# Rotary embedding on one core: first-tile stores in pieces, and a 64 KB partition step with 2 KB table runs

## The chip, the cores and the metric

The kernel runs on one core of a Trainium2 chip. The metric is device time in microseconds (us); a median over several executions is quoted.

## The reference

```python
batch, seq_len, num_heads, head_dim = (8, 2048, 16, 64)
x1, x2 = x_pairs[..., 0], x_pairs[..., 1]       # neighbours in the last axis
out1 = x1 * cos - x2 * sin
out2 = x1 * sin + x2 * cos                      # interleaved again into the last axis
```

Everything is float32: x and the output are 67.1 MB each, cos and sin 0.26 MB each. The arithmetic is a few operations per element, so what counts is moving 134.7 MB in and out.

## The kernel before

x is cut into 16 tiles of 4 MB. A tile has 128 partitions, and each partition holds K = 8 consecutive sequence rows, one run of 32 KB. In a tile, the next partition's run starts 32 KB further on, so a tile is one contiguous stretch of memory.

```python
P, K, NX = 128, 8, 5
x_t = x.rearrange("b (g p k) h d -> b g p k (h d)", p=P, k=K)
out_t = out.rearrange("b (g p k) h d -> b g p k (h d)", p=P, k=K)
cos_t = cos.rearrange("(g p k) c -> p g (k c)", p=P, k=K)      # two 1 KB runs per partition
first_runs = [(0, 1), (1, 2), (2, 4), (4, 8)]
last_runs = [(0, 4), (4, 6), (6, 7), (7, 8)]

def load_runs(i):
    return first_runs if i == 0 else last_runs if i == n - 1 else [(0, K)]

def store_runs(i):
    return last_runs if i == n - 1 else [(0, K)]
# ... cut: halve() casts a piece to bf16 on ScalarE, rotate() is three VectorE operations ...
def widen(j):
    i, k0, k1 = pieces[j]
    nc.scalar.copy(out=tiles[i][:, k0:k1], in_=rotated.pop(j)[:, : k1 - k0])
    g, b = groups[i]
    for r0, r1 in store_runs(i):
        if r1 == k1:
            nc.scalar.dma_start(out=out_t[b, g, :, r0:r1], in_=tiles[i][:, r0:r1])
    if k1 == K and i + NX < n:
        load(i + NX)          # the same buffer: waits until tile i is stored
# ... cut ...
load(0); <cos and sin>; load(1) ... load(4); <build tables>; <pieces in order>
```

Five tile buffers rotate. Loads are issued from SyncE's queue, stores from ScalarE's. The sixth load, tile 5, needs the buffer of tile 0, so it goes out when tile 0 has been stored.

A packet, below, is one record of the DMA trace: one contiguous run moved by one of the 16 DMA engines.

## Time and profile before

| | before |
|---|---|
| device time | 318.54 us, median of 3 (318.48 to 318.76) |
| bytes moved | 134.76 MB |
| VectorE, ScalarE busy | 70%, 73% |
| DMA rate over the span | 425 GB/s |

These lines are from the page of the kernel before; in the lines of part 5, busy time and mean ns of one stand between the bars, and after the second bar the idle time just before and what ended it.

```profile
span 316.9 us, 352 instructions
DVE 223.2 (70%) x111; ACT 230.0 (73%) x73; POOL 0.2 (0%) x4
DMA packets 6451, 134.76 MB, mean 425 GB/s; under 512 B 689, under 2 KB 1201, under 8 KB 1969
...
L75 ACT CAST xh<-xt 128x4096 bf16<-128x4096 f32 (+2 forms) x36 | 116.1, 3224 | 66.9 <-DMA xt<-in_x_dram 61.6
```

No compute engine is full, and ScalarE waits 61.6 us for loads. The windows view of the same kernel shows what fills the time: start:end and length of each stretch, busy time of VectorE, ScalarE and GpSimd, clock, share of the 16 DMA engines, GB/s.

```profile
0.00:3.00 3.00, 0.00 (x0) 1.28 (x1) 0.20 (x4) 1.00 0.38 90
3.00:19.00 16.00, 4.36 (x8) 3.15 (x4) 0.00 (x0) 1.00 1.06 442
19.00:36.00 17.00, 15.26 (x10) 15.15 (x6) 0.00 (x0) 1.00 1.00 432
36.00:98.00 62.00, 58.20 (x26) 59.80 (x17) 0.00 (x0) 1.00 1.00 430
98.00:176.00 78.00, 55.24 (x26) 57.83 (x18) 0.00 (x0) 1.00 1.00 431
176.00:254.00 78.00, 48.74 (x22) 50.27 (x15) 0.00 (x0) 1.00 1.00 432
254.00:308.00 54.00, 39.32 (x21) 39.49 (x13) 0.00 (x0) 1.00 1.00 431
308.00:312.40 4.40, 2.08 (x3) 3.03 (x3) 0.00 (x0) 1.00 0.97 411
312.40:315.20 2.80, 0.00 (x0) 0.00 (x1) 0.00 (x0) 1.00 0.88 361
```

The DMA share is 1.00 from 19 to 308 us. In short windows it can pass 1.00 (1.06 above), so a per cent or two in one such window is not a difference in rate. The Trainium skill, "DMA: Bandwidth & Descriptors", section "Where 436 GB/s comes from", gives 435 GB/s as the ceiling of the fabric; the trace reaches 431.

Two lines more: the first is from SyncE's queue in the timeline (start, length), the other two from the DMA issues (median us from issue to landing).

```profile
59.78 0.33 SPq L70 DMA_DIRECT2D xt<-in_x_dram  x1
...
out_dram<-xt ACTq DMA_DIRECT2D x1, 1024.0 KB, 11.7
out_dram<-xt ACTq DMA_DIRECT2D x2, 512.0 KB, 4.1
```

The sixth load goes out at 59.78 us.

### The profile page before, as it was taken

How to read it: one execution, taken by the hardware profiler on the slowest of the kernel's cores; microseconds unless marked ns; L12 is line 12 of the kernel's file. 1: busy time of each engine (PE TensorE's matmuls, PEld its weight loads, DVE VectorE, ACT ScalarE, POOL GpSimd, SP SyncE). 2: the span in 40 equal slices, each digit the busy share in tenths (PEclk: the TensorE clock that was granted, in tenths of full speed). 3: DMA queues.
4: the chain of work that ended last, by engine and by line, in shares of the span. 5: the costliest groups of instructions: out<-in, count | busy, mean ns of one | idle time of the engine just before them, and what ended most of it. 6: DMA issues, size and time to landing. Idle time of an engine off the chain costs nothing.

```text
span 316.9 us, 352 instructions
## 1 busy us (share of the span) xinstructions
DVE 223.2 (70%) x111; ACT 230.0 (73%) x73; POOL 0.2 (0%) x4
## 2 busy tenths in 40 slices
DVE  0189999999999596693967939588440999999112
ACT  4078899999998692976949679495803999997322
POOL 0000000000000000000000000000000000000000
DMA  7999999999999999999999999999999999999997
GB/s 304 424 463 405 455 397 401 459 438 422 455 405 463 397 460 401 459 414 448 443 418 455 405 459 405 455 405 459 418 443 447 414 428 430 424 433 439 442 414 302
DMA packets 6451, 134.76 MB, mean 425 GB/s; under 512 B 689, under 2 KB 1201, under 8 KB 1969
## 3 DMA queue, kind: packets, MB, share of 16 engines
q1 hardware_dynamic: 3712, 67.63, 50.1%
q10 hardware_dynamic: 2736, 67.11, 49.1%
q14 instruction: 3, 0.02, 0.0%
HBM read 67.63 MB, written 67.11 MB: 425 GB/s over the span
## 4 chain that ended last, share of the span: by engine, by line
DMA 62%; ACT 26%; DVE 4%; issue 3%; another core or an unknown queue 2%; SPq 1%; ACTq 1%
DMA xt<-in_x_dram 31%; DMA out_dram<-xt 28%; ACT xt L105 14%; ACT xh L75 12%; DMA sin_sb<-in_sin_dram 4%; DVE xh L100 1%; DVE xh L95 1%; DVE qt L94 1%; SPq L70 1%; ACTq L109 1%; DVE s_tab L121 0%; SPq L115 0%; DVE s_tab L122 0%; ACTq L105 0%
## 5 line engine op out<-in xcount | busy, mean ns | idle before, releaser
L75 ACT CAST xh<-xt 128x4096 bf16<-128x4096 f32 (+2 forms) x36 | 116.1, 3224 | 66.9 <-DMA xt<-in_x_dram 61.6
L105 ACT CAST xt<-xh 128x4096 f32<-128x4096 bf16 (+2 forms) x36 | 116.0, 3223 | 14.8 <-DVE xh L100 14.4
L94 DVE TENSOR_TENSOR qt<-xh,s_tab 128x4096 bf16<-128x4096 bf16 (+2 forms) x36 | 74.0, 2055 | 71.2 <-ACT xh L75 70.3
L100 DVE TENSOR_TENSOR xh<-xh,qt 128x4096 bf16<-128x4096 bf16 (+2 forms) x36 | 74.0, 2055 | 1.2
L95 DVE TENSOR_TENSOR xh<-xh,c_tab 128x4096 bf16<-128x4096 bf16 (+2 forms) x36 | 74.0, 2055 | 1.2
L121 DVE CAST s_tab<-sin_sb 128x512 bf16<-128x512 f32 x1 | 0.5, 453 | 14.4 <-DMA sin_sb<-in_sin_dram 14.4
L75 ACT ACT_TABLE_LOAD x1 | 1.3, 1283 | 0.7 <-PEq L147 0.7
L123 DVE CAST c_tab<-cos_sb 128x1024 bf16<-128x1024 f32 x1 | 0.7, 684 | 0.0
L122 DVE TENSOR_SCALAR s_tab<-sin_sb 128x512 bf16<-128x512 f32 x1 | 0.4, 442 | 0.0
L147 POOL MEMSET const-bfloat16-1.0<- 128x1 bf16 x1 | 0.1, 101 | 0.0
L147 POOL MEMSET const-uint8-127<- 128x1 uint8 x1 | 0.1, 101 | 0.0
L147 POOL MEMSET const-float32-0.0<- 128x1 f32 x1 | 0.1, 98 | 0.2 <-issue 0.2
L147 POOL MEMSET const-float32-1.0<- 128x1 f32 x1 | 0.1, 98 | 0.0
## 6 DMA issues: line engine op xcount, KB each, us to landing
out_dram<-xt ACTq DMA_DIRECT2D x15, 4096.0 KB, 38.6
xt<-in_x_dram SPq DMA_DIRECT2D x14, 4096.0 KB, 26.6
xt<-in_x_dram SPq DMA_DIRECT2D x2, 2048.0 KB, 16.3
xt<-in_x_dram SPq DMA_DIRECT2D x4, 512.0 KB, 24.1
xt<-in_x_dram SPq DMA_DIRECT2D x2, 1024.0 KB, 19.9
out_dram<-xt ACTq DMA_DIRECT2D x1, 2048.0 KB, 17.6
out_dram<-xt ACTq DMA_DIRECT2D x1, 1024.0 KB, 11.7
out_dram<-xt ACTq DMA_DIRECT2D x2, 512.0 KB, 4.1
```

The source lines that it names most:

```text
L70: nc.sync.dma_start(out=tiles[i][:, k0:k1], in_=x_t[b, g, :, k0:k1])
L75: nc.scalar.copy(out=halved[j][:, : k1 - k0], in_=tiles[i][:, k0:k1])
L94: nc.vector.tensor_tensor(out=rows(qt), in0=rows(xh), in1=tab(s_tab), op=mult)
L95: nc.vector.tensor_tensor(out=rows(xh), in0=rows(xh), in1=tab(c_tab), op=mult)
L100: nc.vector.tensor_tensor(out=xh3, in0=xh3, in1=q_swap, op=add)
L105: nc.scalar.copy(out=tiles[i][:, k0:k1], in_=rotated.pop(j)[:, : k1 - k0])
L109: nc.scalar.dma_start(out=out_t[b, g, :, r0:r1], in_=tiles[i][:, r0:r1])
L121: nc.vector.tensor_copy(out=s2[:, :, 0], in_=sin_flat)
L122: nc.vector.tensor_scalar_mul(s2[:, :, 1], sin_flat, -1.0)
L123: nc.vector.tensor_copy(out=c_tab.rearrange("p g k (i j) -> p (g k i) j", j=2), in_=cos_sb.rearrange("p g c -> p (g c)").to_broadcast([P, ...
L147: nc = _bacc.Bacc("TRN2", target_bir_lowering=False, num_devices=1)
```

## The change

The intent: start storing the first tile before all of it is done, and read each partition's table rows in one run of 2 KB. To get the second, a partition now holds 16 consecutive rows of a batch row, and two tiles are interleaved over them.

```diff
-    x_t = x.rearrange("b (g p k) h d -> b g p k (h d)", p=P, k=K)
-    out_t = out.rearrange("b (g p k) h d -> b g p k (h d)", p=P, k=K)
-    cos_t = cos.rearrange("(g p k) c -> p g (k c)", p=P, k=K)
-    sin_t = sin.rearrange("(g p k) c -> p g (k c)", p=P, k=K)
+    x_t = x.rearrange("b (p g k) h d -> b g p k (h d)", p=P, k=K)
+    out_t = out.rearrange("b (p g k) h d -> b g p k (h d)", p=P, k=K)
+    cos_t = cos.rearrange("(p k) c -> p (k c)", p=P)
+    sin_t = sin.rearrange("(p k) c -> p (k c)", p=P)
 ...
     def store_runs(i):
-        return last_runs if i == n - 1 else [(0, K)]
+        return load_runs(i)
 ... (cut: the same tables without the g axis)
```

A partition's run of x stays 32 KB, but its neighbour's now starts 64 KB further on.

More of the change, by code (lines that the diff above doesn't have):

```diff
@@ L41 @@
     hpool = ctx.enter_context(tc.tile_pool(name="hpool", bufs=1))
-    cos_sb = consts.tile([P, G, K * D2], fp32)
-    sin_sb = consts.tile([P, G, K * D2], fp32)
+    cos_sb = consts.tile([P, G * K * D2], fp32)
+    sin_sb = consts.tile([P, G * K * D2], fp32)
     c_tab = consts.tile([P, G, K, D], bf16)
@@ L119 @@
         s2 = s_tab.rearrange("p g k (i j) -> p (g k i) j", j=2)
-        sin_flat = sin_sb.rearrange("p g c -> p (g c)")
-        nc.vector.tensor_copy(out=s2[:, :, 0], in_=sin_flat)
-        nc.vector.tensor_scalar_mul(s2[:, :, 1], sin_flat, -1.0)
+        nc.vector.tensor_copy(out=s2[:, :, 0], in_=sin_sb)
+        nc.vector.tensor_scalar_mul(s2[:, :, 1], sin_sb, -1.0)
         nc.vector.tensor_copy(
             out=c_tab.rearrange("p g k (i j) -> p (g k i) j", j=2),
-            in_=cos_sb.rearrange("p g c -> p (g c)").to_broadcast([P, G * K * D2, 2]),
+            in_=cos_sb.to_broadcast([P, G * K * D2, 2]),
         )
```

## The prediction

> **What bounds the kernel now.** The DMA engines, nearly without a gap. The page gives 134.76 MB at a mean of 425 GB/s over a span of 316.9 us; ScalarE is busy 73%, VectorE 70%. The windows view shows a DMA share of 1.00 and 430 to 432 GB/s in each of 19:36, 36:98, 98:176, 176:254 and 254:308 us, and 431 GB/s over 3:315.2. The Trainium skill, "DMA: Bandwidth & Descriptors", section "Where 436 GB/s comes from", puts the fabric ceiling of the 16 engines at 435 GB/s; the trace agrees, at 99% of it. The waits view shows ScalarE waiting 61.6 us for loads and the load queue 242 us for stores: both sides wait for DMA. From 36 to 98 us the chain of waits runs through ScalarE alone, but the DMA share there is 1.00 too, so this costs nothing.
>
> Outside saturation lie only the first 3 us (90 GB/s) and the end: 308:312.4 at 411 GB/s, 312.4:315.2 at 361, and 1.7 us after the last byte. Against 431 GB/s about 2.4 us are lost at the head and 2.4 us at the end. This is all that any reordering could win.
>
> **What the change does.**
> 1. The first tile's single 4 MB store, issued at 35.9 us, becomes four, at about 19, 22, 27 and 36 us (the ends of its widening copies in the timeline). But from 19 to 36 us the DMA engines already run at 432 GB/s on loads. Some 2 MB of stores move forward and push 2 MB of loads back; the sum is the same. The sixth load, issued at 59.8 us once this store has landed, should go out 5 to 10 us earlier. Gain at the end: about 0. Cost: three more issues of 0.34 us on ScalarE's queue, where there is slack (12.7 us of waiting right after 98 us).
> 2. The tables come in 256 packets of 2 KB instead of 512 of 1 KB: 0.5 MB, 1.2 us of DMA time at 431 GB/s. I estimate at most 0.2 us saved.
> 3. Not named in the words of the change: a partition's runs of x and out stay 32 KB, but the step between partitions becomes 64 KB instead of 32 KB; tiles are no longer one contiguous 4 MB. The same page, "Latency and other measured facts", reports a 3% loss at an HBM row pitch of 512 KiB and far more at 2 MiB; 64 KiB is below what it lists. I expect no loss; no run has shown it yet.
>
> Instructions, shapes and order on VectorE are unchanged.
>
> **Predicted time:** 318.3 us, 8 times in 10 between 317.0 and 319.8. Chances: faster by over 2%: 1%; within 2%: 96%; slower by over 2%: 3%.
>
> **What the profile would show.** Span near 316.7. The windows between 19 and 308 us at 430 to 432 GB/s; 134.76 MB moved. Four first-tile stores from about 19 us. The sixth load issued nearer 50 us. ScalarE's wait for loads within 10 of 61.6 us. Packets under 2 KB fewer by about 512. The last load lands 7 to 9 us before the last byte.
>
> **What would make it wrong.** A steady rate below 425 GB/s at the 64 KB step (each 1% lost costs 3 us), or one nearer 435 (2 to 3 us won). Or fewer bytes of stores are queued when the last load lands (3 MB now), so that the DMA engines idle during the last chain of 4.3 us (308.1 to 312.4): 1 to 2 us lost.

## More of the kernel before

A 4 MB tile is 128 packets of 32 KB; a piece of one sequence row per partition (512 KB) is 128 packets of 4 KB. Every transfer ends with a 4-byte completion packet on each engine.

## The result, and the profile after

| | before | after |
|---|---|---|
| device time, median | 318.56 us (318.48 to 318.76, 4 runs) | 318.86 us (318.71 to 319.03, 4 runs) |
| ratio | | 1.0009, 95% interval 0.9991 to 1.0026 |
| profiled span | 316.9 us | 316.9 us |

A ratio is the mean time of one kernel's fast runs over that of the other's from the same rounds, so it is not quite the ratio of the medians quoted. The interval includes 1: no difference is shown.

The page of the changed kernel, the lines that answer to those above:

```profile
span 316.9 us, 352 instructions
DVE 223.2 (70%) x111; ACT 230.3 (73%) x73; POOL 0.2 (0%) x4
DMA packets 6626, 134.76 MB, mean 425 GB/s; under 512 B 736, under 2 KB 736, under 8 KB 2016
...
L76 ACT CAST xh<-xt 128x4096 bf16<-128x4096 f32 (+2 forms) x36 | 116.1, 3225 | 67.7 <-DMA xt<-in_x_dram 61.1
```

The windows view of the changed kernel, the same stretches and columns:

```profile
0.00:3.00 3.00, 0.00 (x0) 1.28 (x1) 0.20 (x4) 1.00 0.40 68
3.00:19.00 16.00, 3.95 (x7) 2.70 (x3) 0.00 (x0) 1.00 1.05 438
19.00:36.00 17.00, 14.21 (x10) 14.54 (x7) 0.00 (x0) 1.00 0.98 419
36.00:98.00 62.00, 58.25 (x27) 59.74 (x18) 0.00 (x0) 1.00 1.01 434
98.00:176.00 78.00, 56.44 (x25) 58.44 (x17) 0.00 (x0) 1.00 1.00 432
176.00:254.00 78.00, 48.16 (x22) 50.26 (x15) 0.00 (x0) 1.00 1.00 432
254.00:308.00 54.00, 40.14 (x21) 40.30 (x13) 0.00 (x0) 1.00 1.00 430
308.00:312.40 4.40, 2.08 (x3) 2.67 (x3) 0.00 (x0) 1.00 0.98 416
312.40:315.20 2.80, 0.00 (x0) 0.37 (x1) 0.00 (x0) 1.00 0.88 360
```

Bytes, busy times and rates are the same; the 1 KB packets are gone. The 419 in 19:36 is an effect of the window's edges: with each packet's bytes spread over its own duration, 7.34 MB were moved in that stretch before and 7.32 MB after.

The timeline of SyncE's queue and the DMA issues of the changed kernel did not do what was predicted:

```profile
63.59 0.33 SPq L71 DMA_DIRECT2D xt<-in_x_dram  x1
...
out_dram<-xt ACTq DMA_DIRECT2D x4, 512.0 KB, 10.1
out_dram<-xt ACTq DMA_DIRECT2D x2, 1024.0 KB, 20.3
```

The sixth load goes out 3.8 us later than before, at 63.59 us, although its buffer's store was started 16 us earlier (first piece at 19.47 us). The median time to landing of the 512 KB stores is 10.1 us instead of 4.1, because two of the four are now first-tile pieces.

The trace's packet records, cumulated by queue (MB moved by each time), show why:

```
us                      24     28     32     36     40     44     48     60
before, load queue    9.14  10.87  12.60  14.33  15.94  16.78  17.30  20.27
before, store queue   0.00   0.00   0.00   0.00   0.00   0.75   1.96   4.19
after,  load queue    8.95  10.48  12.02  13.56  15.10  16.63  17.90  21.50
after,  store queue   0.08   0.28   0.47   0.65   0.84   1.04   1.40   2.99
```

From 24 to 44 us the store queue of the changed kernel gets about 0.19 MB in 4 us, the load queue 1.53 MB: one ninth of the total, and a 4 KB packet beside a 32 KB packet is 4/36, one ninth. Between 28 and 36 us, 91 load packets of 32 KB and 91 store packets of 4 KB start. The two queues take turns packet by packet, and a turn is worth what its packet holds. The Trainium skill, same page, section "Queues, rings and completion order", says that each engine goes round robin between its queues at packet granularity; this trace agrees, 91 to 91. (The page gives a packet as typically 9 to 17 descriptors. Here one turn is one packet record, one partition's run; how many descriptors make up a record the trace does not show.)

So the four pieces of the first tile were complete at 34.7, 45.8, 57.9 and 63.0 us, the whole tile of before at 59.4 us: the early pieces did arrive earlier, but the last one, which frees the buffer, arrived later.

In the kernel before, both queues carried 32 KB packets once the store began. Between 44 and 48 us the store queue got 1.21 MB of 1.73: 32 of its packets started beside 16 of the load queue, whose other 16 turns went to 4-byte completion packets. A completion packet takes a turn too.

### The profile page after: what moved, and what is told of

Its sections match the earlier page's. It is cut to its first block, busy times and chain, and to the rows that moved or that the text cites. A ratio compares the mean times of both kernels' runs of the same rounds, so it can differ in the third digit from the quotient of the medians.

```text
span 316.9 us, 352 instructions
## 1 busy us (share of the span) xinstructions
DVE 223.2 (70%) x111; ACT 230.3 (73%) x73; POOL 0.2 (0%) x4
## 4 chain that ended last, share of the span: by engine, by line
DMA 72%; ACT 16%; DVE 4%; issue 3%; another core or an unknown queue 2%; SPq 1%; ACTq 1%
DMA out_dram<-xt 37%; DMA xt<-in_x_dram 32%; ACT xt L106 9%; ACT xh L76 7%; DMA sin_sb<-in_sin_dram 4%; DVE xh L101 1%; DVE xh L96 1%; DVE qt L95 1%; SPq L71 1%; ACTq L110 1%; SPq L116 0%; DVE s_tab L121 0%; DVE s_tab L122 0%; DVE c_tab L123 0%
## 5 line engine op out<-in xcount | busy, mean ns | idle before, releaser
L76 ACT CAST xh<-xt 128x4096 bf16<-128x4096 f32 (+2 forms) x36 | 116.1, 3225 | 67.7 <-DMA xt<-in_x_dram 61.1
## 6 DMA issues: line engine op xcount, KB each, us to landing
out_dram<-xt ACTq DMA_DIRECT2D x4, 512.0 KB, 10.1
```

The lines of the kernel that those rows point to most:

```text
L76: nc.scalar.copy(out=halved[j][:, : k1 - k0], in_=tiles[i][:, k0:k1])
```

## The experiments

All of them are correct unless marked. "By 19 us" means the megabytes that packet records show as moved by then.

**1. The store pieces alone**, on the layout of before.

```diff
     def store_runs(i):
-        return last_runs if i == n - 1 else [(0, K)]
+        return load_runs(i)
```

> Kernel before plus the first tile's store in four pieces; 32 KB step between partitions kept. Theory (the two DMA queues take turns packet by packet, so a 4 KB store packet gets one turn against a 32 KB load packet): the store queue moves at 4/36 = 11% of the total while 4 KB packets stand at its head, about 0.2 MB per 4 us from 24 to 44 us; the sixth load goes out at 63 to 65 us, later than the 59.8 us of before, and the total time is that of before within 0.2 us. Sine rows land at 14.4 us as before. Rival (the 64 KB step or the table layout delayed the sixth load): it goes out at or before 59.8 us here.

Measured: 319.28 us (319.24 to 319.85, 5 runs) against 318.67; ratio 1.0022, interval 1.0009 to 1.0036. From its SyncE timeline:

```profile
64.65 0.33 SPq L70 DMA_DIRECT2D xt<-in_x_dram  x1
```

The sixth load is late without the new layout, and the store queue moves 0.19 MB per 4 us between 24 and 44 us (90 load packets of 32 KB beside 93 store packets of 4 KB from 28 to 36 us). So the pieces delay it, not the step. Two expectations missed: the sine rows landed at 15.2 us, not 14.4 (14.5 in the repetition, experiment 10), and the time rose by 0.6 us, not 0.2 (which did repeat).

**2. The new layout alone**: the changed kernel with the first tile stored whole.

```diff
     def store_runs(i):
-        return load_runs(i)
+        return last_runs if i == n - 1 else [(0, K)]
```

> The changed kernel with the first tile stored whole: 64 KB step and 2 KB table runs alone. Theory: the head is slower by about 0.4 us (first 1 MB of loads, 4 KB packets, mean over 200 ns instead of 190; sine rows land at 14.8 to 15.0 us), the steady windows stay at 430 to 432 GB/s, the sixth load goes out at about 60 us, and the time is 0.2 to 0.5 us over before. Rival (0.3 us of the changed kernel is noise, or comes from the store pieces): the time is that of before within 0.15 us.

Measured: 318.97 us (318.83 to 319.25, 5 runs) against 318.67; ratio 1.0009, interval 0.9996 to 1.0021. From its SyncE timeline and its waits view (us in total, times, longest):

```profile
60.16 0.33 SPq L71 DMA_DIRECT2D xt<-in_x_dram  x1
...
DVE s_tab L121 <- DMA sin_sb<-in_sin_dram: 14.8, 1, 14.8
```

The sixth load is back at 60 us. The head, the first microseconds of the kernel, is slower: 6.93 MB by 19 us instead of 7.03, which is 0.23 us at 431 GB/s (about 0.4 was expected), and the 4 KB packets of the first 1 MB took 210 ns on average instead of 191. The 0.3 us in the total agrees in sign and size, but the interval includes 1.

**3. Smaller load packets beside the store pieces**: the changed kernel with tiles 1 to 4 loaded in quarters, 8 KB packets.

```diff
+        quarters = [(0, 2), (2, 4), (4, 6), (6, 8)]
-        return first_runs if i == 0 else last_runs if i == n - 1 else [(0, K)]
+        return first_runs if i == 0 else quarters if i < NX else last_runs if i == n - 1 else [(0, K)]
```

(Stores of tiles 1 to 4 stay whole.)

> The changed kernel with tiles 1 to 4 loaded in four pieces each, so that the load packets which compete with the first stores are 8 KB instead of 32 KB. Packet-turn theory: the 4 KB store packets now get 4/12 = 33% of the rate, about 0.55 to 0.6 MB per 4 us instead of 0.2, the 8 KB ones half; the first tile's last piece lands near 50 us, and the sixth load goes out when the early loads are done, near 50 us instead of 63.5. Rival (a store piece is slow by itself, by its completion or its 4 KB packets): the store rate stays near 0.2 MB per 4 us and the sixth load near 63 us. Total time: within 1 us of the changed kernel, as the DMA engines stay full.

Measured: 319.89 us (one run, state unknown). From its SyncE timeline:

```profile
49.54 0.33 SPq L72 DMA_DIRECT2D xt<-in_x_dram  x1
```

From 24 to 28 us the store queue moved 0.56 MB and the load queue 1.14 MB: a share of 33%, as 4/12 demands, where it was 11%. The sixth load went out at 49.54 us, 14 us sooner. Same 4 KB store packets, same sizes, another neighbour: a store piece is not slow by itself. The total time did not gain from the earlier load. It was 1.03 us over the changed kernel's 318.86, just outside the 1 us expected. The smaller load packets alone account for about 0.8 us of that: an estimate from the usual duration of each packet size, summed over all packets and divided by 16 engines.

**4. The first tile loaded whole**, on the kernel before.

```diff
     def load_runs(i):
-        return first_runs if i == 0 else last_runs if i == n - 1 else [(0, K)]
+        return last_runs if i == n - 1 else [(0, K)]
```

> Kernel before with the first tile loaded whole (32 KB packets) instead of in four pieces. The tables land after that tile anyway, so the early pieces buy no compute. If the slow head is many small packets: 0.2 to 0.6 us faster, with the sine rows earlier than 14.4 us. If the head is a cost of first touching the memory, whatever the packets: same time within 0.2 us.

Measured: 318.45 us (318.36 to 318.87, 5 runs) against 318.67; ratio 0.9995, interval 0.9982 to 1.0007. The median is 0.2 us lower, the low end of what was expected, but the interval includes 1. By 19 us 7.04 MB instead of 7.03, and the sine rows landed at 14.5 us: nothing that shows was won at the head. At the 32 KB step the small first packets cost no time that shows. They bring no rotation forward either, since the tables land after that tile (the sine rows at 14.4 us); only the first casts to bf16 run early.

**5, 6, 7. A copy in place of the kernel**: the same tiles, buffers and queues, the loaded tile stored unchanged, no tables; with a step between partitions of 32, 64 and 512 KB. Their outputs are wrong, which doesn't matter for the times.

```diff
-    <tables, halve, rotate, widen>
+    for i in range(n):
+        nc.scalar.dma_start(out=out_t[b, g], in_=tiles[i])
+        if i + NX < n:
+            load(i + NX)
 (512 KB: "(p i k) c -> i p k c" on the (b s) rows)
```

> Wrong on purpose: x is loaded and stored unchanged in whole tiles through the same two queues and five buffers, no tables, no arithmetic; 32 KB step. Theory (the packets' time fills the kernel): 4096 packets of 32 KB at 1213 ns on 16 engines are 310.5 us; with the 2 us of head, 1 to 1.5 us of slow first packets and the end, 316.5 to 317.5 us, so all the arithmetic, tables and pieces of the kernel before cost only 1 to 2 us. Rival (the waits for ScalarE or for buffers cost more than the windows show): under 315 us.

> The same copy, wrong on purpose, with the 64 KB step. Theory (the step only slows the first packets): 0.1 to 0.5 us over the copy with the 32 KB step, steady windows equal. Rival (the step costs bandwidth): more than 1 us over it, spread over the span. If the 0.3 us of the changed kernel was noise: equal within 0.1 us.

> The same copy, wrong on purpose, with a 512 KB step (a partition holds 128 consecutive rows, over batch rows). The Trainium skill's page on DMA reports 3% less for that row pitch in copies from HBM to HBM; if this holds for a single pass through SBUF: 3% over the copy with 32 KB, about 326 us. If only the first packets on fresh memory are slow: head excess 2 to 8 times that of the 32 KB step and 317 to 320 us.

| step | median us (range, runs) | ratio to before, 95% interval |
|---|---|---|
| 32 KB | 316.78 (316.65 to 317.0, 6) | 0.9927, 0.9887 to 0.9966 |
| 64 KB | 317.02 (316.47 to 317.1, 6) | 0.9930, 0.9890 to 0.9970 |
| 512 KB | 320.01 (319.22 to 323.61, 4) | 1.0051, 0.9975 to 1.0126 |

Before had a median of 318.67 in these rounds; one of its 11 runs, at 323.13, widens the intervals.

The 32 KB copy is the floor of this design, and the kernel before is 1.9 us above it. The packet durations account for that: at their usual durations (the median for each size) the kernel before's packets take 312.7 us of 16 engines, the copy's 310.6. Of the 2.1 us between them 1.5 are the tables (512 packets of 46 ns over 16 engines), and nearly all of the rest is the smaller packets of the first and last tile. No cost is left over for the arithmetic.

The ranges of the 32 and 64 KB copies overlap, so a loss from the 64 KB step itself is not shown. The windows view of the 512 KB copy (no VectorE or ScalarE columns) shows that even that step does not lower the steady rate:

```profile
36.00:98.00 62.00, 0.00 (x0) 1.00 1.00 431
98.00:176.00 78.00, 0.00 (x0) 1.00 1.00 431
176.00:254.00 78.00, 0.00 (x0) 1.00 1.00 432
254.00:308.00 54.00, 0.00 (x0) 1.00 0.98 424
```

It is 1.0% over the 32 KB copy (320.01 to 316.78), not 3%. In its profiled run (320.59 us), packets that took longer than usual for their size make 3.0 us of all engines instead of 1.6, and from 285 us to the last byte the engines are idle for 2.7 us on average instead of 0.5, as some finish before others. Its median lies at the edge of the 317 to 320 us that the second expectation gave, but the first 8 us lost 0.7 us, as in the 32 KB copy, and not 2 to 8 times as much: the cause that it named did not show. The Trainium skill, same page, section "Latency and other measured facts", has 207 against 214 GB/s for that pitch in copies from HBM to HBM; this pass through SBUF loses less.

**8. Head and tail in larger packets**, on the kernel before: the version that the packet turns point to.

```diff
     def load_runs(i):
-        return first_runs if i == 0 else last_runs if i == n - 1 else [(0, K)]
+        return [(0, 4), (4, 8)] if i == n - 1 else [(0, K)]
```

> Kernel before with the first tile loaded whole, and the last tile loaded in two halves (16 KB packets) instead of in 16, 8, 4 and 4 KB runs; compute and stores of the last tile stay in pieces. Packet-turn theory: the last load, no longer in 4 and 8 KB packets against 32 KB store packets, lands 3 to 6 us earlier than 308.1 us; then stores alone fill the end, and the last stretch runs at about 420 GB/s instead of 361. Time: 0.3 to 0.9 us under before. If the last chain of compute then ends too late, no gain.

Measured: 318.57 us (318.33 to 319.27, 6 runs) against 318.67; ratio 0.9984, interval 0.9943 to 1.0024. The last load landed at 290.0 us instead of 307.7: packet turns again, in the other direction, since the 4 and 8 KB load packets of the last tile had been standing against 32 KB store packets. An engine had 32 load packets of that tile before and has 16 now; with a 32 KB store packet of 1213 ns after each, 16 turns fewer are about 19 us (an estimate), and 17.7 were measured. But the windows of its end are those of before:

```profile
308.00:312.40 4.40, 0.00 (x0) 0.00 (x0) 0.00 (x0) 1.00 0.96 406
312.40:315.20 2.80, 0.00 (x0) 0.00 (x0) 0.00 (x0) 1.00 0.86 350
```

No compute runs there any more and every store was issued by 304 us, yet the rate is no higher than 411 and 361 GB/s. So the last chain of compute is not what holds the end. In the packet records the 16 engines finish one after another (the last dozen store packets end between 314.85 and 315.51 us); what else keeps that stretch under 431 GB/s was not taken apart. The expected 0.3 to 0.9 us did not come.

**9. The new layout with the first tile loaded and stored whole.**

```diff
     def load_runs(i):          # in the changed kernel
-        return first_runs if i == 0 else last_runs if i == n - 1 else [(0, K)]
+        return last_runs if i == n - 1 else [(0, K)]
```

> The changed layout (64 KB step, 2 KB table runs) with the first tile loaded and stored whole. Theory (the head loses 0.25 us because its first 1 MB goes in 4 KB packets at the 64 KB step): the loss vanishes, 7.0 MB or more are moved by 19 us, sine rows at 14.3 to 14.6 us, and the time is 0 to 0.4 us under before. Rival (the step costs at the head whatever the packets): 6.9 MB by 19 us and 0.2 to 0.4 us over before.

Measured: 318.66 us (318.54 to 319.02, 5 runs) against 318.60; ratio 0.9997, interval 0.9984 to 1.0009. By 19 us 7.12 MB, and the sine rows landed at 14.2 us: the loss at the head is gone. So it takes both, the 64 KB step and the 4 KB first packets. The time is level with before: about 0.06 us above in the medians, which neither expectation named.

**10, 11. The store pieces alone and the changed kernel, once more.**

> The run with the store pieces on the 32 KB step once more, unchanged, since it came out 0.6 us over before, more than the whole change. If that belongs to this kernel: 0.4 to 0.8 us over before again, and slow load packets again between 66 and 80 us (0.5 us of all engines in the first run). If it was that chip or that run: within 0.3 us of before, without those slow packets. The sixth load goes out near 64 us in both cases.

> The changed kernel itself, beside the others on one chip. If its 0.3 us over before is real: 0.2 to 0.5 us again. Sixth load at 63 to 65 us.

| | median us (range, runs) | before | ratio, 95% interval | sixth load |
|---|---|---|---|---|
| pieces alone | 319.44 (318.74 to 319.94, 6) | 318.60 | 1.0018, 1.0004 to 1.0032 | 63.19 us |
| changed kernel | 318.80 (318.62 to 319.22, 6) | 318.60 | 1.0004, 0.9991 to 1.0016 | 63.58 us |

The marker repeats. The pieces alone are slower by 0.2% in two sets of rounds. In the first profile that time lay in slow packets between 66 and 80 us (about 0.5 us of all engines). The second had none of them, and instead its engines ended raggedly: 2.1 us idle between 308 us and the last byte, against 0.7 in the kernel before and 0.8 in the first profile. The loss is repeatable and its place is not; its cause stays open. The changed kernel does not show it: its 0.2 and 0.3 us over before lie inside both intervals.

## Why the prediction was right or wrong

**Right: the time, and its main reason.** 318.86 us was measured against 318.3 predicted, inside 317.0 to 319.8. The DMA engines were full and the bytes were the same, so reordering could move almost nothing. The copy confirms it: 1.9 us above it is all that the kernel has, and the packets alone account for that. The closeness to 0.6 us is not a merit of the details: the prediction leaned 0.2 us to the fast side (318.3 against 318.54), the medians lean 0.3 us to the slow side, neither clear of noise, and two effects that it did not foresee offset each other (see "Where that loss went").

**Right in size: the tables.** 512 packets of 46 ns became 256 of 84 ns. Over 16 engines that is 0.13 us saved, under the 0.2 us allowed.

**Wrong: "Some 2 MB of stores move forward" and "The sixth load ... should go out 5 to 10 us earlier".** By 36 us only 0.65 MB had been stored, and the sixth load went out 3.8 us later. The prediction gave no rule for how the two queues share the engines, but 2 MB could move forward only if the stores got far more than they did; the queues share by packets, and 4 KB against 32 KB is one ninth. Experiment 1 shows that the pieces do it, experiment 3 that the neighbour's packet size sets the share. In the changed kernel it cost nothing that shows in the total, for the reason given: the engines were full either way. (The 0.2% of the pieces alone stays unexplained.)

**Wrong in part: "I expect no loss" from the 64 KB step.** In every run with that step and 4 KB first packets (the changed kernel twice, experiments 2 and 3), 6.87 to 6.93 MB were moved by 19 us instead of 7.03, a loss of 0.2 to 0.4 us (the 6.87 is experiment 3, whose smaller load packets are part of it; the other three are at 0.24). This is what is left after the 0.13 us saved by the tables, which lie in the same stretch. Without the small first packets the loss is gone (experiment 9). The steady rate did not suffer.

**Where that loss went.** In the two profiled runs, the sum of all packet durations over 16 engines is 314.50 us before and 314.62 after. Three terms make up most of the difference: the usual durations rose by 0.07 us (0.20 for the pieces, less 0.13 for the tables); slow packets in the first 8 us rose from 0.51 to 0.96; slow load packets between 36 and 60 us fell from 0.60 to 0.20. The last is when stores begin: in the kernel before, load packets lost 0.5 us at 38 to 40 us. The other profiles agree: in all five with the first tile stored whole (before, experiments 2, 4, 8 and 9) load packets lost 0.5 to 0.9 us between 36 and 40 us, in all five with it in pieces none there and at most 0.3 between 40 and 60 (experiment 3 lost 0.3 at 22 to 24 us instead). Why the slow packets come when stores begin is not shown.

**Loose as a bound: 2.4 us at the end, part of "all that any reordering could win".** One reordering that wins nothing does not refute a bound, but experiment 8 put the last load 18 us forward and won nothing there, and the copy stays only 1.9 us below the kernel, 1.5 of them the tables. (By the packet records the last byte of the kernel before landed at 315.7 us, so about 1.2 us followed it, not 1.7.)

**The other signs.** ScalarE waited 61.1 us for loads, predicted within 10 of 61.6. The last load landed 7.6 us before the last byte, as predicted (308.1 and 315.7 us). Packets under 2 KB fell by 465, not 512, because the three additional stores brought 48 completion packets. From 19 to 308 us the windows held 430 to 434 GB/s except 19:36, which is an edge effect.

## What to carry to other kernels

When the DMA share is 1.00 from end to end, first build the plain copy with the same tiles: its time is what reordering can reach at best, and here it left 1.9 us of 318.7, most of it for tables that have to be read anyway. Before cutting a transfer into pieces, look at what stands in the other queue: small packets beside large ones get a share by packet size, so although the first pieces arrive early, the last can arrive later than the whole would have (63.0 against 59.4 us here), and it is the last that frees the buffer. A layout change should be read for the address step that it brings along, and the first microseconds are where such a step may show.

## What the Trainium skill lacked or had wrong

- "DMA: Bandwidth & Descriptors", section "Queues, rings and completion order": the round robin by packet is stated, but not what follows for a kernel author. Here one packet record is as large as a partition's contiguous run, up to 32 KB, the shares were 1/9 for 4 KB beside 32 KB and 1/3 for 4 KB beside 8 KB, and a 4-byte completion packet took a turn like any other (16 of the load queue's 32 turns between 44 and 48 us in the kernel before).
- Same page, its bandwidth table is for transfers issued from GpSimd; durations by packet size on the SyncE and ScalarE queues are missing. Here 4, 8, 16 and 32 KB took 159, 309, 611 and 1213 ns on one engine: about 9 ns per packet and 150 ns for each 4 KB.
- Same page, section "Latency and other measured facts": a 512 KiB row pitch is given with 3% loss for HBM to HBM. Here it was 1.0% of the time, with 431 to 432 GB/s in the windows from 36 to 254 us, and 64 KB showed no loss in a copy.
- Same page, section "Where 436 GB/s comes from", says that about 358 GB/s binds between HBM and SBUF. One core alone moved 431 GB/s here; the "HBM Reference", section "Specifications (TRN2)", already says that a core streaming alone is above that share.
- No page has slow packets at the start of a stream: 0.4 to 0.8 us of all engines in the first 8 us, 0.8 to 1.0 us with 4 KB packets at the 64 KB step, and 0.5 to 1.2 us on the load queue when whole 32 KB packets of stores begin (the kernel before at 38 us, the copies at 14 to 20 us).
